# One stage of a diffusion layer: the adaLN products of a small vector with 1 MB weight slabs, in split fp32r or in plain fp32 on four column groups

## The chip, the cores and the metric

The kernel runs on one core of one Trainium2 chip. A core has a matrix engine (TensorE; PE for its matmuls and PEld for its weight loads in the profile), a vector engine (DVE), a scalar engine (ACT), GpSimd (POOL) and a queue engine (SP) that here issues nearly all transfers (DMAs). Operands lie in an on-chip memory of 128 partitions (SBUF), and matmuls write to a second one, the accumulators (PSUM). The engines run side by side, and each takes its own instructions in program order. The metric is the device time of one execution in microseconds (us), lower is better.

## The reference

The layer normalises the latent tokens `x` and the context tokens `ctx`, scales and shifts them by vectors that come from the conditioning vectors `c` and `c_ctx` (adaLN), and then does a projection, a neighbourhood attention, a short convolution and an output projection. What matters here is how scale and shift come about:

```python
def adaln(cond, w_ada, b_ada):
    m = jax.nn.silu(cond) @ w_ada + b_ada
    return jnp.split(m, 3, axis=-1)

    shift, scale, gate = adaln(c, w_ada, b_ada)
    shift_c, scale_c, gate_c = adaln(c_ctx, w_ada, b_ada)
    h = rmsnorm(x, norm_g) * (1 + scale[:, None]) + shift[:, None]
    hc = rmsnorm(ctx, norm_g) * (1 + scale_c) + shift_c
```

Here `cond` has 1024 entries, `w_ada` is 1024 x 3072 in float32, `x` is 1024 x 1024 and `ctx` 256 x 1024. Everything is float32; the kernel does its large matmuls on operands split into a high and a low part of a reduced type (fp32r).

## The kernel before

All engines are held to an order written out by hand: each instruction on PE, ACT, DVE and POOL, and each transfer of SP, is issued in the order of the program text (`strict`, line 549). So a wait at the head of one engine's queue holds everything behind it on that engine.

The stage in question is the first, lines 549 to 922. It makes the modulated activations `hh[k]`, `hl[k]` (high and low part, transposed, k = 0 to 7 blocks of 128 features) and, at the same time, the first three column groups of the projection (`first_columns`, line 723: nine matmuls of 512 columns per call, which read the high part in the first six and the low part in the last three). Two blocks k belong to one m (m = 0 to 3). For each m there are two slabs of `w_ada`, (m, 0) for shift and (m, 1) for scale, of 1024 rows x 256 columns, 1 MB each (`load_slab`, line 557). Slabs of m = 0 lie in the later places of `hh[6]`, `hh[7]`. All later ones share three buffers with the tag `slab`, and so do, in this order, the context tokens `xc` (line 835), the table `rw8` (line 736, called at line 857 as `gains_load`) and the table `rg` (line 749, in `gains`, called at line 847). A new tile takes the first buffer that comes free, so `slab` buffers pass on in this order: the buffer of (2,1) to `xc`, that of (3,0) to `rw8`, that of (3,1) to `rg`.

`products(m, j)` (line 642) multiplies silu(c), silu(c_ctx) with slab (m, j), in 8 row blocks `kt` of 128 rows, the vectors as the stationary operand and 256 columns of the slab moving. The result is 2 or 4 rows of a PSUM tile `mods[m]`, one of only two buffers named `tr`, which the transposes of x (`transposed`, line 698) and of ctx take in turn as well. Slabs (0,0), (0,1) and (1,0) are multiplied in plain fp32. For the other five, ACT (once DVE) casts the slab to a high part `slabh`, DVE subtracts to get a low part `slabl` (`cast_slab`, `rest_of`, `split`, lines 624 to 640), and PE multiplies both parts in fp32r with `c4`, whose four columns are the high and low parts of the two vectors. A slab's buffer is free once it has been split.

`row_copy` (line 653) copies the rows from PSUM; `modulation` (line 659) transposes them with four small PE transposes back into `mods[m]`, and DVE adds biases and writes the per-feature scale and shift `ab`. `turn(half, k, on)` (line 704) then makes `hh[k]`, `hl[k]` from the transposed x: ACT writes the high part `h`, ACT or DVE the full value `hw`, DVE subtracts.

In the loop over m from 1 to 3 (line 840) the order on PE is `first_columns`, `transposed`, `products(m+1, 0)`, `first_columns`, `products(m+1, 1)`, `transposed`, a third of `first_columns`, `modulation(m+1)`, the rest. `gains` stands on POOL at the head of m = 2: it scales the rope tables in `rw8` by the q and k gains into `rg`, and SP stores that (`rope_d`). Behind it on POOL stand the two powers for the norm of `xc` (`root`, line 617), for which DVE's `norm(xc)` (lines 863 and 864) waits; behind that on DVE stand `split_chunk(6)`, `modulation(3)` and the low part of `turn(1,5)`. Behind the store on SP stand the eight loads of the next weight chunks (`chunk_load(CQ, k)`, lines 848 to 900), whose casts (line 899) stand on ACT ahead of `turn(1,6)` (line 842 with m = 3).

`keep_clock(n)` (line 590) issues n idle matmuls on zeroes. After the stage, the kernel goes on to projection tiles (`pacc`, line 297), attention and the output projection.

Of the kernel before, what the change touches and what calls it, by code (L numbers as in the profile page):

```python
# [10 lines left out]
F32 = mybir.dt.float32  # L11
F32R = mybir.dt.float32r
BF16 = mybir.dt.bfloat16
AF = mybir.ActivationFunctionType
ALU = mybir.AluOpType
# [4 lines left out]
P = 128  # L20
# [3 lines left out]
KT = D // P  # L24
# [15 lines left out]
def body(tc, es, x, ctxt, w_ada, b_ada, w_in, q_g, k_g, rpbr, w_out, vecs, cst, out):  # L40
# [21 lines left out]
    pe, act, dve, pool = every = [ordered(e) for e in (nc.tensor, nc.scalar, nc.vector, nc.gpsimd)]  # L62
    sp = ordered(nc.sync)

    def sbuf(name, side=None, bufs=1):
        kw = {} if side is None else {"side": side}
        return tc.tile_pool(name=name, bufs=bufs, reuse_waits="tile", **kw)
# [43 lines left out]
    cp = es.enter_context(sbuf("cp"))  # L111
    ci = cp.tile([P, P + 2], F32, name="ci")
    ident = ci[:, 0:P]
# [15 lines left out]
    def fill_up(pool_, n):  # L129
        pool_.tile([P, n // 4], F32, name="pad")  # L130

    c2 = cp.tile([P, KT, 2], F32, name="c2")
    ab = cp.tile([P, KT, 4], F32, name="ab")
    ng, bsh, bsc = vecT[:, 16:24], vecT[:, 24:32], vecT[:, 32:40]
# [8 lines left out]
    def place(k, shape, dtype, name):  # L143

        return hpool.tile(shape, dtype, name=name, tag=f"h{k}")
# [7 lines left out]
    cvp = hs.enter_context(sbuf("cvp", side="right"))  # L153
    bp = hs.enter_context(sbuf("bp", side="right"))
    b1 = bp.tile([P, KT], F32, name="b1")
    fill_up(bp, 192)
    hcs = ExitStack()
    hcp = hcs.enter_context(sbuf("hcp"))
# [388 lines left out]
        return ps0.tile([P, 512], F32, name="tr", tag="tr", bufs=2)  # L547

    strict[:] = every + [sp]
    xx, slabs, highs, lows, chunks, mods, pts = {}, {}, {}, {}, {}, {}, {}  # L550

    def load_x(ts):
        for t in ts:
# [36 lines left out]
    def keep_clock(n):  # L590

        for _ in range(n):
            pe.matmul(acc0[2][1], warm[:, :P], warm, start=True, stop=True)
# [4 lines left out]
    dve.tensor_copy(vecT, pv[:, :nvec])  # L598
    act.activation(c2[:].rearrange("p k a -> p a k"), vecT[:, 0:16].rearrange("p (a k) -> p a k", a=2), AF.Silu)
    dve.tensor_scalar(b1, bsc, 1.0, None, ALU.add)  # L600
    c4 = cp.tile([P, KT, 4], F32R, name="c4")
    act.copy(c4[:, :, 0:2], c2)
    c0 = cp.tile([P, KT, 8], F32, name="c0")[:, :, 0:4]
    pool.memset(c0[:, :, 2:4], 0.0)
    act.copy(c0[:, :, 0:2], c2)
    keep_clock(7)
    dve.tensor_tensor(c4[:, :, 2:4], c2, c4[:, :, 0:2].bitcast(F32), ALU.subtract)

    sums = {}

# [10 lines left out]
    def norm(xtile, n):  # L621
        dve.tensor_scalar(xtile, xtile, sums[n], None, ALU.mult)

    def cast_slab(m, j, part, cast):

        if part == 0:
            highs[j] = hcp.tile([P, KT, 256], F32R, name="slabh", tag="AB"[j])
            lows[j] = place(6 + j, [P, KT, 256], F32R, "slabl")
        rows = slice(4 * part, 4 * part + 4)
        cast(highs[j][:, rows], slabs[m, j][:, rows])  # L630

    def rest_of(m, j, part):

        rows = slice(4 * part, 4 * part + 4)
        dve.tensor_tensor(lows[j][:, rows], slabs[m, j][:, rows], highs[j][:, rows].bitcast(F32), ALU.subtract)

    def split(m, j, part):

        cast_slab(m, j, part, act.copy)
        rest_of(m, j, part)  # L640

    def products(m, j, kts=range(KT), parts=(0, 1)):

        if m not in mods:
            mods[m] = tr()
        rows = mods[m][:4 if m else 2, 256 * j:256 * j + 256]
        split_ = [(c4, highs[j]), (c4, lows[j])] if (m, j) >= (1, 1) else [(c0 if m else c2, slabs[m, j])]
        for i, (c, part) in enumerate(split_):
            for kt in kts if i in parts else ():
                pe.matmul(rows, c[:, kt], part[:, kt], start=(i == 0 and kt == 0 and j == 0),  # L650
                          stop=(i == len(split_) - 1 and kt == KT - 1 and j == 1), skip_group_check=True)

    def row_copy(m):
        n = 4 if m else 2
        rw = cvp.tile([4, 512], F32, name="rw", tag="ub", bufs=2)
        (act.copy if m else dve.tensor_copy)(rw[:n], mods[m][:n])
        return rw[:n]

    def modulation(m, rw):

        n, ks = 4 if m else 2, slice(2 * m, 2 * m + 2)
        pm = mods[m]
        for j in range(2):
            for i in range(2):
                pe.transpose(pm[:, n * (2 * j + i):n * (2 * j + i + 1)], rw[:, 256 * j + i * P:256 * j + (i + 1) * P],
                             ident[:n, :n])
        both = lambda v: v[:, ks].rearrange("p (k o) -> p k o", o=1).broadcast_to([P, 2, 2])
        abk = ab[:, ks].rearrange("p k (w j) -> p j k w", w=2)
        pm = pm[:, 0:4 * n].rearrange("p (j k w) -> p j k w", j=2, k=2)
        dve.tensor_tensor(abk[:, 0], pm[:, 0, :, 0:2], both(bsh), ALU.add)  # L670
        dve.tensor_tensor(abk[:, 1], pm[:, 1, :, 0:2], both(b1), ALU.add)
        if n > 2:
            for j in range(2):
                dve.tensor_tensor(abk[:, j], abk[:, j], pm[:, j, :, 2:4], ALU.add)
        dve.tensor_tensor(abk[:, 1], abk[:, 1], both(ng), ALU.mult)

    def modulated(hi, lo, ps, k, w, on, between=None):
# [100 lines left out]
    rw = row_copy(0)  # L778
# [26 lines left out]
        norm(xx[t - 1], t - 1)  # L805
    first_columns(0, 1)
    norm(xx[7], 7)
    cast_slab(1, 1, 0, act.copy)
    cast_slab(1, 1, 1, dve.tensor_copy)
    rest_of(1, 1, 0)  # L810
    rest_of(1, 1, 1)
    products(1, 0, range(6))
    transposed(1, 0)
    products(1, 0, range(6, KT))
    turn(1, 0, act)
    load_slab(2, 1)
    load_chunks([4, 5])
    products(1, 1, parts=(0,))
    products(1, 1, range(4), (1,))
    transposed(1, 1)  # L820
    products(1, 1, range(4, KT), (1,))
    load_slab(3, 0)
    split_chunk(2)
    turn(1, 1, act)
    first_columns(1, 0)
    rw = row_copy(1)
    split_chunk(3)
    split(2, 0, 0)
    load_slab(3, 1)
    load_chunks([6, 7])  # L830
    transposed(0, 2)
    modulation(1, rw)
    turn(0, 2, dve)
    split(2, 0, 1)
    xc = sl.tile([P, 2, D], F32, name="xc", tag="slab", bufs=3)
    sp.dma_start(xc, ctxt[0].rearrange("(i p) d -> p i d", p=P))
    first_columns(1, 1)
# [2 lines left out]
    for m in range(1, 4):  # L840
        k, new, last = 2 * m, m < 3, m == 3
        turn(1, k, act)
        if m == 1:
            split(2, 1, 0)
            split(2, 1, 1)
        if m == 2:
            gkc = gains(tables)
            ch = [chunk_load(CQ, k) for k in range(4)]
        first_columns(0, k)
        transposed(0, k + 1)  # L850
        if new:
            products(m + 1, 0)
        turn(0, k + 1, dve)
        if m == 1:
            split(3, 0, 0)
            split(3, 0, 1)
            tables = gains_load()
        if m == 2:
            for i in range(2):
                square(xc[:, i], i)  # L860
            root(0)
            root(1)
            norm(xc[:, 0], 0)
            norm(xc[:, 1], 1)
        if last:
            transposed_ctx(0)
            ch[4] = chunk_split(ch[4])
            turn_ctx(0)
            spread = bias_tables()
            next(spread)  # L870
        first_columns(1, k)
        if new:
            split_chunk(k + 2)
            products(m + 1, 1)
            rw = row_copy(m + 1)
        transposed(1, k + 1)
        first_columns(0, k + 1, (0,))
        if last:
            transposed_ctx(1)
        if new:  # L880
            modulation(m + 1, rw)
        turn(1, k + 1, act)
        if new:
            split_chunk(k + 3)
        if m == 1:
            split(3, 1, 0)
        if last:
            turn_ctx(1)
        first_columns(0, k + 1, (1, 2))
        if new:  # L890
            transposed(0, k + 2)
            if m == 2:
                more_h(range(6, KT))
            turn(0, k + 2, dve)
        if m == 1:
            split(3, 1, 1)
        if m == 2:
            ch.append(chunk_load(CQ, 4))
            ch[0:4] = map(chunk_split, ch[0:4])
            ch += [chunk_load(CQ, k) for k in (5, 6, 7)]  # L900
        if last:
            group0 = conv_group(0, {u: acc0[n] for n, u in enumerate((CU, CBG, CCG))})
            next(group0)
            do_acts()
            do_dves()
            transposed_ctx(2)
            ch[5] = chunk_split(ch[5])
            turn_ctx(2)
            first_columns(1, k + 1, (0,))
            transposed_ctx(3)  # L910
            ch[6] = chunk_split(ch[6])
            first_columns(1, k + 1, (1,))
            ch[7] = chunk_split(ch[7])
            turn_ctx(3)
            first_columns(1, k + 1, (2,))
        else:
            first_columns(1, k + 1)
            transposed(1, k + 2)
# [200 lines left out]
    def both(v, n, part=slice(0, 31)):  # L1119

        lo, hi = span(2 * (n % 4))
        return v[:, :, part.start * 12:min(part.stop, hi - lo) * 12]
# [150 lines left out]
    for n in range(NT + 3):  # L1273


        p, t = divmod(n, NB)
# [51 lines left out]
        if 1 < n <= NT + 1:  # L1328
            m, r = n - 2, (n - 2) % NB
# [69 lines left out]
    with sbuf("att") as ap, psum("psb") as psb:  # L1399
# [6 lines left out]
        for n in range(len(TICKS)):  # L1406
            h, g = divmod(n, 4)
# [7 lines left out]
            if ready:  # L1415
                p = ready.pop()
# [150 lines left out]
```

## Time and profile before

| what | us |
| --- | --- |
| median of 3 runs | 630.24 |
| fastest and slowest of them | 628.92, 630.98 |
| span of the profiled execution | 629.7 |
| PE busy in it | 621.4 |
| DVE, ACT, POOL busy | 433.5, 325.5, 78.0 |
| first projection tile (`pacc`) starts at | 77.65 |

The profile is of one execution, taken on the same core; times in its views are counted from the start of its span. A row of the timeline has the start, the length, the engine, the line of the code, the operation, the tile written and the tiles read, the shapes, how many like instructions are merged, and in brackets how long the engine had been idle and what released it. "SPq" is the issue of a transfer. Nearly every instruction bears line 55, that of the helper that keeps the order; so rows are told apart by their tiles. The chain of waits is followed back from the last instruction; its rows have a start, a length and the work. A plain fp32 matmul shows up as two weight loads and two matmuls, called two passes below; an fp32r one as one of each.

### The profile page before, as it was taken

The numbers are of one execution on the slowest core, as the hardware profiler recorded it, in microseconds if no ns is written. First come the engines' busy times: TensorE is split into PE (matmuls) and PEld (weight loads), VectorE is DVE, ScalarE is ACT, GpSimd is POOL, SyncE is SP. The second block draws the span as 40 slices with busy tenths as digits, with TensorE's granted clock in tenths as the row PEclk, the third lists the DMA queues.
The fourth block names the chain that finished last, engine by engine and source line by source line (L and its number), as shares of the span: only waits on it lengthen the run. The fifth ranks groups of instructions, "written<-read, shape, count | busy, mean of one in ns | idle before, by whom it ended". The sixth has DMA issues, their size and how long they took to land.

```text
span 629.7 us, 9816 instructions
## 1 busy us (share of the span) xinstructions
PE 621.4 (99%) x3391; PEld 530.9 (84%) x3392; DVE 433.5 (69%) x889; ACT 325.5 (52%) x712; POOL 78.0 (12%) x102
## 2 busy tenths in 40 slices
PE   8999999999999999999999999999999999999998
PEld 3577899999999999888888888888878788878887
DVE  1887858866867855478897888987998755495111
ACT  4777835424625545346576568567774844451000
POOL 1305014123123222100000000000000002004200
PEclk9999999999999999999999999999999999999999
DMA  8983738967784994886566472857441235973631
GB/s 318 346 288 119 187 97 275 280 200 242 250 272 149 303 321 167 312 258 221 151 213 179 153 236 70 267 199 256 125 136 61 73 95 160 338 230 117 218 101 51
DMA packets 104030, 126.45 MB, mean 201 GB/s; under 512 B 10689, under 2 KB 70553, under 8 KB 102700
## 3 DMA queue, kind: packets, MB, share of 16 engines
q1 hardware_dynamic: 97516, 114.24, 55.3%
q10 hardware_dynamic: 6208, 11.05, 5.7%
q0 software_dynamic: 256, 0.54, 0.3%
q8 instruction: 27, 0.44, 0.3%
q14 instruction: 23, 0.19, 0.1%
HBM read 89.04 MB, written 39.04 MB: 203 GB/s over the span
## 4 chain that ended last, share of the span: by engine, by line
PE 88%; DMA 5%; ACT 3%; DVE 2%; issue 1%; ACTq 1%; SPq 1%; DVEq 0%
PE pu L55 25%; PE pacc L55 21%; PE po L55 8%; PE acc L55 6%; PE pout L76 4%; PE pout L74 4%; PE pout L75 4%; PE tr L55 4%; PE cacc L55 4%; PE pss L55 3%; DMA woraw<-in_w_out 2%; PE pc L55 2%; PE pmx L55 2%; DMA xx<-in_x 2%; DMA xr<-in_x 1%; PE trA L55 1%
## 5 line engine op out<-in xcount | busy, mean ns | idle before, releaser
L55 PE MATMUL pu<-h,uh 128*128 128x512 f32 x544 | 169.9, 394 | 0.3 <-ACT zs L55 0.3
L55 PE MATMUL pacc<-w,h 128*128 128x384 f32 x768 | 138.4, 337 | 0.0
L55 PEld LDWEIGHTS pacc<-w,h 128*128 128x128 f32 x768 | 132.7, 188 | 0.2
L55 PEld LDWEIGHTS pu<-h,uh 128*128 128x128 f32 x544 | 97.7, 188 | 17.4 <-ACT zs L55 0.6
L55 PE MATMUL pu<-h,ul 128*128 128x512 f32 x272 | 106.6, 392 | 0.0
L55 PEld LDWEIGHTS pu<-h,ul 128*128 128x128 f32 x272 | 51.1, 188 | 11.2
L55 POOL TENSOR_TENSOR ss<-ss,few 128x4 f32<-128x4 f32 (+1 forms) x40 | 41.9, 1049 | 124.8 <-DVE ss L55 124.8
L74 PE MATMUL pout<-woh,yh 128*128 128x512 f32 (+2 forms) x136 | 51.7, 380 | 1.0 <-ACT yh L1471 1.0
L75 PE MATMUL pout<-wol,yh 128*128 128x512 f32 (+2 forms) x136 | 51.6, 380 | 0.0
L76 PE MATMUL pout<-woh,yl 128*128 128x512 f32 (+2 forms) x136 | 50.9, 380 | 0.0
L55 PE MATMUL acc<-h,w 128*128 128x512 f32 x144 | 38.1, 405 | 0.8 <-ACT h L55 0.8
L55 ACT ACTIVATE sq<-pacc 128x256 f32<-128x256 f32 x32 | 12.4, 387 | 47.7 <-PE pacc L55 47.2
L55 ACT ACTIVATE phc<-sc 128x512 fp32r<-128x512 f32 x32 | 20.3, 634 | 30.1 <-DVE sc L55 30.1
L55 DVE TENSOR_REDUCE rm<-pmx 128x2 f32<-128x256 f32 (+1 forms) x33 | 13.7, 416 | 29.8 <-PE pmx L55 29.4
L55 DVE TENSOR_TENSOR mx<-mx,sb 128x372 f32<-128x372 f32 (+2 forms) x64 | 31.9, 498 | 1.9
L55 ACT COPY mg<-pmx 128x256 f32<-128x256 f32 (+1 forms) x33 | 12.0, 365 | 39.1 <-PE pmx L55 33.9
L55 PE MATMUL po<-phl,v 128*65 128x276 f32 (+2 forms) x192 | 32.0, 269 | 0.0
L55 DVE TENSOR_REDUCE ss<-sq 128x4 f32<-128x260 f32 (+1 forms) x40 | 15.6, 391 | 23.7 <-ACT sq L55 23.6
L55 ACT ACTIVATE qn<-pacc,ss 128x64 f32<-128x64 f32 x128 | 30.1, 332 | 3.0 <-POOL ss L55 3.0
L55 PEld LDWEIGHTS acc<-h,w 128*128 128x128 f32 x144 | 25.5, 188 | 6.5 <-ACT h L55 1.2
L74 PEld LDWEIGHTS pout<-woh,yh 128*128 128x128 f32 x136 | 25.6, 188 | 6.1 <-ACT yh L1471 1.5
L76 PEld LDWEIGHTS pout<-woh,yl 128*128 128x128 f32 x136 | 25.6, 188 | 5.1 <-DVE yl L1472 0.4
(159 smaller groups left out, 1158.7 us busy)
## 6 DMA issues: line engine op xcount, KB each, us to landing
uraw<-in_w_in SPq DMA_DIRECT2D x34, 256.0 KB
q_d<-qs SPq DMA_DIRECT2D x32, 256.0 KB
k_s<-k_d SPq DMA_DIRECT2D x8, 1024.0 KB
q_s<-q_d SPq DMA_DIRECT2D x16, 512.0 KB
wr<-in_w_in SPq DMA_DIRECT2D x40, 192.0 KB
slab<-in_w_ada SPq DMA_DIRECT2D x6, 1024.0 KB
v_d<-vs SPq DMA_DIRECT2D x20, 260.0 KB
v<-v_d SPq DMA_DIRECT2D x16, 325.0 KB
```

The lines of the kernel that those rows point to most:

```text
L55: i = emit(*a, **kw)
L74: i = pe.matmul(ps, ah, bh, start=first, stop=False)
L75: pe.matmul(ps, ah, bl, start=False, stop=False)
L76: pe.matmul(ps, al, bh, start=False, stop=last)
```

## The change

All eight slabs are multiplied in plain fp32, unsplit. The stationary operand is `c32`: 32 columns, of which two hold the vectors and 30 are zero. Row block `kt` writes to output partitions 32·(kt mod 4) to 32·(kt mod 4) + 31, so consecutive row blocks go to four different groups of 32 partitions, and each group holds a partial sum over two row blocks. `row_copy` copies all 128 partitions; the four partial sums are added in `modulation` by four matmuls with a selector, two columns of the constant `ci` with ones at partitions of one parity, in place of the four transposes. Casts and subtractions of the slabs go, with them `c4`, `c0`, `slabh`, `slabl`. The products of slabs (1,0) and (1,1), which stood in pieces between transposes, now stand whole ahead of both transposes.

```diff
+    fill_up(cp, 128)
+    c32 = cvp.tile([P, KT, 32], F32, name="c32", tag="cv", bufs=2)
+    pool.memset(c32, 0.0)
+    act.copy(c32[:, :, 0:2], c2)
...
-        rows = mods[m][:4 if m else 2, 256 * j:256 * j + 256]
-        split_ = [(c4, highs[j]), (c4, lows[j])] if (m, j) >= (1, 1) else [(c0 if m else c2, slabs[m, j])]
-        for i, (c, part) in enumerate(split_):
-            for kt in kts if i in parts else ():
-                pe.matmul(rows, c[:, kt], part[:, kt], start=(i == 0 and kt == 0 and j == 0),
-                          stop=(i == len(split_) - 1 and kt == KT - 1 and j == 1), skip_group_check=True)
+        for kt in range(KT):
+            g = 32 * (kt % 4)
+            pe.matmul(mods[m][g:g + 32, 256 * j:256 * j + 256], c32[:, kt], slabs[m, j][:, kt],
+                      start=(j == 0 and kt < 4), stop=(j == 1 and kt >= 4), skip_group_check=True)
...
+        for n in range(4):
+            pe.matmul(pm[:, 2 * n:2 * n + 2], rw[:, n * P:(n + 1) * P], ci[:, P:P + 2], start=True, stop=True)
...
-        if n > 2:
-            for j in range(2):
-                dve.tensor_tensor(abk[:, j], abk[:, j], pm[:, j, :, 2:4], ALU.add)
...
-    cast_slab(1, 1, 0, act.copy)
-    cast_slab(1, 1, 1, dve.tensor_copy)
-    rest_of(1, 1, 0)
-    rest_of(1, 1, 1)
-    products(1, 0, range(6))
+    products(1, 0)
+    products(1, 1)
     transposed(1, 0)
-    products(1, 0, range(6, KT))
     turn(1, 0, act)
     load_slab(2, 1)
     load_chunks([4, 5])
-    products(1, 1, parts=(0,))
-    products(1, 1, range(4), (1,))
     transposed(1, 1)
-    products(1, 1, range(4, KT), (1,))
...
         turn(0, k + 1, dve)
         if m == 1:
-            split(3, 0, 0)
-            split(3, 0, 1)
             tables = gains_load()
```

The other six calls of `split` go in the same way.

More of the change, by code (lines that the diff above doesn't have):

```diff
@@ L549, in body @@
     strict[:] = every + [sp]
-    xx, slabs, highs, lows, chunks, mods, pts = {}, {}, {}, {}, {}, {}, {}
+    xx, slabs, chunks, mods, pts = {}, {}, {}, {}, {}
     def load_x(ts):
@@ L600, in body @@
     dve.tensor_scalar(b1, bsc, 1.0, None, ALU.add)
[L601 to L605, printed above, removed]
+    fill_up(cp, 128)
+    c32 = cvp.tile([P, KT, 32], F32, name="c32", tag="cv", bufs=2)
+    pool.memset(c32, 0.0)
+    act.copy(c32[:, :, 0:2], c2)
     keep_clock(7)
-    dve.tensor_tensor(c4[:, :, 2:4], c2, c4[:, :, 0:2].bitcast(F32), ALU.subtract)
     sums = {}
@@ L622, in norm @@
         dve.tensor_scalar(xtile, xtile, sums[n], None, ALU.mult)
[L624 to L642, printed above, removed]
+    def products(m, j):
         if m not in mods:
             mods[m] = tr()
-        rows = mods[m][:4 if m else 2, 256 * j:256 * j + 256]
-        split_ = [(c4, highs[j]), (c4, lows[j])] if (m, j) >= (1, 1) else [(c0 if m else c2, slabs[m, j])]
-        for i, (c, part) in enumerate(split_):
-            for kt in kts if i in parts else ():
-                pe.matmul(rows, c[:, kt], part[:, kt], start=(i == 0 and kt == 0 and j == 0),
-                          stop=(i == len(split_) - 1 and kt == KT - 1 and j == 1), skip_group_check=True)
+        for kt in range(KT):
+            g = 32 * (kt % 4)
+            pe.matmul(mods[m][g:g + 32, 256 * j:256 * j + 256], c32[:, kt], slabs[m, j][:, kt],
+                      start=(j == 0 and kt < 4), stop=(j == 1 and kt >= 4), skip_group_check=True)
@@ L653, in row_copy @@
     def row_copy(m):
[L654 to L657, printed above, removed]
+        rw = cvp.tile([P, 512], F32, name="rw", tag="ub", bufs=2)
+        (act.copy if m else dve.tensor_copy)(rw, mods[m])
+        return rw
     def modulation(m, rw):
-        n, ks = 4 if m else 2, slice(2 * m, 2 * m + 2)
+        ks = slice(2 * m, 2 * m + 2)
         pm = mods[m]
-        for j in range(2):
-            for i in range(2):
-                pe.transpose(pm[:, n * (2 * j + i):n * (2 * j + i + 1)], rw[:, 256 * j + i * P:256 * j + (i + 1) * P],
-                             ident[:n, :n])
+        for n in range(4):
+            pe.matmul(pm[:, 2 * n:2 * n + 2], rw[:, n * P:(n + 1) * P], ci[:, P:P + 2], start=True, stop=True)
@@ L667, in modulation @@
         both = lambda v: v[:, ks].rearrange("p (k o) -> p k o", o=1).broadcast_to([P, 2, 2])
         abk = ab[:, ks].rearrange("p k (w j) -> p j k w", w=2)
-        pm = pm[:, 0:4 * n].rearrange("p (j k w) -> p j k w", j=2, k=2)
-        dve.tensor_tensor(abk[:, 0], pm[:, 0, :, 0:2], both(bsh), ALU.add)
-        dve.tensor_tensor(abk[:, 1], pm[:, 1, :, 0:2], both(b1), ALU.add)
-        if n > 2:
-            for j in range(2):
-                dve.tensor_tensor(abk[:, j], abk[:, j], pm[:, j, :, 2:4], ALU.add)
+        pm = pm[:, 0:8].rearrange("p (j k w) -> p j k w", j=2, k=2)
@@ L675, in modulation @@
+        dve.tensor_tensor(abk[:, 0], pm[:, 0], both(bsh), ALU.add)
+        dve.tensor_tensor(abk[:, 1], pm[:, 1], both(b1), ALU.add)
         dve.tensor_tensor(abk[:, 1], abk[:, 1], both(ng), ALU.mult)
@@ L827, in body @@
     split_chunk(3)
-    split(2, 0, 0)
     load_slab(3, 1)
@@ L833, in body @@
     turn(0, 2, dve)
-    split(2, 0, 1)
     xc = sl.tile([P, 2, D], F32, name="xc", tag="slab", bufs=3)
@@ L842, in body @@
         turn(1, k, act)
-        if m == 1:
-            split(2, 1, 0)
-            split(2, 1, 1)
         if m == 2:
@@ L884, in body @@
             split_chunk(k + 3)
-        if m == 1:
-            split(3, 1, 0)
         if last:
@@ L894, in body @@
             turn(0, k + 2, dve)
-        if m == 1:
-            split(3, 1, 1)
         if m == 2:
```

## The prediction

> **What bounds the kernel now.** I read the page's head first, then the chain of waits in order of time, then the timeline of the first 80 us.
>
> ```profile
> span 629.7 us, 9816 instructions
> ...
> PE 621.4 (99%) x3391; PEld 530.9 (84%) x3392; DVE 433.5 (69%) x889; ACT 325.5 (52%) x712; POOL 78.0 (12%) x102
> ```
>
> PE is busy almost throughout, and the other engines have room. So work taken from DVE and ACT is worth something only where PE waits for them, and a new wait of PE lengthens the run by its whole length. The chain shows where each microsecond of the first stage goes:
>
> ```profile
> 4.99 9.87 DMA xx<-in_x
> ...
> 25.24 6.60 PE tr L55 x40
> 31.84 2.07 PE acc L55 x9
> 33.91 0.77 PE tr L55 x8
> 34.68 2.27 PE acc L55 x9
> 36.95 0.44 PE tr L55 x4
> 37.39 2.54 PE acc L55 x9
> 39.92 2.26 PE tr L55 x20
> 42.19 2.06 PE acc L55 x9
> ...
> 54.19 2.26 PE tr L55 x20
> 56.45 2.06 PE acc L55 x9
> 58.51 2.31 PE tr L55 x20
> ...
> 68.49 0.91 PE tr L55 x8
> ...
> 77.65 12.51 PE pacc L55 x72
> ```
>
> "acc" is `first_columns`; "tr" holds transposes and products. Up to about 15 us the chain is the load of x; from 25 us it is PE alone. A "tr x20" is four transposes (0.44 as at 36.95) and sixteen product passes, so one split slab costs PE 2.26 - 0.44 = 1.82 (after (2,1) and (3,1): 2.31 - 0.44 = 1.87). Last comes what waits beside PE and is nearly late already:
>
> ```profile
> 40.59 2.36 DVE L55 TENSOR_TENSOR slabl<-slab,slabh 128x1024 fp32r<-128x1024 f32 x2
> 42.98 0.37 SPq L55 DMA_DIRECT2D xc<-in_ctx  x1
> 44.31 2.35 DVE L55 TENSOR_TENSOR slabl<-slab,slabh 128x1024 fp32r<-128x1024 f32 x2
> 46.70 0.34 SPq L55 DMA_DIRECT2D rw<-in_q_norm_g  x1
> 47.56 0.42 SPq L55 DMA_DIRECT2D rw<-in_cst  x1
> 52.04 1.35 DVE L55 TENSOR_TENSOR slabl<-slab,slabh 128x1024 fp32r<-128x1024 f32 x1
> 53.47 5.95 POOL L55 TENSOR_TENSOR rg<-rw 128x512 f32<-128x512 f32 x4 [1.16 <-DVE slabl L55]
> 59.44 0.33 SPq L55 DMA_DIRECT2D rope_d<-rg  x1
> 59.81 8.39 SPq L55 DMA_DIRECT2D wr<-in_w_in  x8
> 59.98 1.58 DVE L55 TENSOR_SCALAR xc<-xc,xss 128x1024 f32<-128x1024 f32 x2 [2.07 <-POOL xss L55]
> 65.11 2.24 ACT L55 CAST w<-wr 128x384 fp32r<-128x384 f32 x4 [0.41 <-DMA wr<-in_w_in]
> 67.93 0.77 ACT L55 ACTIVATE hw<-tr,ab 128x512 f32<-128x512 f32 x1
> 68.75 0.42 PEld L55 LDWEIGHTS tr<-ci,xc 128*128 128x128 f32 x4
> ```
>
> Three hand-overs of a slab buffer are visible: the second low part of (2,1) ends at 42.95 and `xc` is issued at 42.98; that of (3,0) ends at 46.66 and the loads of `rw8` start at 46.70; that of (3,1) ends at 53.39 and POOL starts on `rg` at 53.47. From there one chain runs on: `rg` ends at 59.42, the store goes at 59.44, the chunk loads behind it, their casts on ACT start at 65.11 after a wait for the DMA, then `turn(1,6)`, whose last ACT part ends at 68.70, and at 68.75 PE takes the context transposes, which need the `tr` buffer that it frees. PE came from 68.49 without a break, so this side chain has about 0.1 us of slack.
>
> **The change, part by part.**
>
> *The price S of a slab on PE.* Four groups of output partitions at once is an operation that the trace doesn't show. These rows bound it:
>
> ```profile
> L55 PE MATMUL tr<-slab,c x48: 378/379/380, 6.7 to 29.1; 128*2 128x256 f32 x32, 128*4 128x256 f32 x16
> ...
> 6.71 7.07 PE L55 MATMUL tr<-slab,c 128*2 128x256 f32 x32
> ...
> 27.69 1.05 ACT L55 CAST slabh<-slab 128x1024 fp32r<-128x1024 f32 x1 [2.61 <-DMA slab<-in_w_ada]
> ...
> 28.64 0.77 ACT L55 ACTIVATE h<-tr,ab 128x512 fp32r<-128x512 f32 x1
> ...
> 34.27 0.40 PE L55 MATMUL tr<-ci,rw 4*128 4x4 f32 x4
> ```
>
> The first row is from the view by tile, the others from the timeline. 32 plain passes take 7.07; a pass by itself takes 379 ns, so 31 intervals fill 6.69, 0.216 each. Sixteen in a row without overlap are S = 3.45; four at a time S = 0.86. Both passes of one row block use the same 32 output partitions and follow each other directly. If PE keeps their order, only the second pass of a block can run beside the first of the next: nine steps of 0.216, S = 1.94. I take 2.0, since two passes per block are what the row shows, and keep 0.86 and 3.45 as ends. That is no better than the 1.82 of a split slab. The Trainium skill, "TensorE: Matmul & The Clock Gate", Part 3, has matmuls in different column groups overlap, a pack lasting as long as one matmul and 4 ns for each further tile, but also says that matmuls start and end in strict order; no run here shows either yet. Taken for all four groups, it gives the lower end.
>
> *`modulation`.* Four transposes (0.33 of the 0.77 at 33.91) become four plain matmuls, eight passes. At the transposes' pace they take 0.66, at that of full 128-row transposes (0.44 for four) 0.88: I take +0.45 for each m. Two small DVE additions go and nothing on PE waits for them.
>
> *Products ahead of the transposes.* (1,1) lands by 27.69, where ACT's wait for it ends; (1,0) can be multiplied from 25.24 and ends before that for S up to 2.45. Then come S, `transposed(1,0)` 0.44, `h` 0.77, `hw` 0.77 and `transposed(1,1)` 0.44, which needs the `tr` buffer that `turn(1,0)` reads (the other is `mods[1]`), and 0.15 for hand-overs. `first_columns(1,0)` starts at 30.26 + S instead of 31.84: S - 1.58. The pieces of products that covered this wait are gone.
>
> *Up to `products(3,0)`.* To 37.39: 2.07 + 0.44 + 0.78 + 2.07 + 0.44 = 5.80 for 5.55, +0.25. At 37.39 a block took 2.54 for 2.07, waiting for DVE, which no longer subtracts slabs: -0.46. Then (2,0) S - 1.82, (2,1) S - 1.87, `modulation(2)` +0.45, (3,0) S - 1.82. Sum: 4S - 6.85. With S = 2.0, +1.15: `products(3,0)` ends at 57.6 instead of 56.45.
>
> *Casts and subtractions removed.* Ten subtractions of 1.2 us and ten casts leave DVE and ACT. Beyond the 0.46, PE waited for none of them, so they are worth nothing more. Products of m = 0 end before the load of x at 14.86 in any case: nothing.
>
> *Who frees the buffers.* This decides. A slab's buffer came free when DVE had split it; now when PE has multiplied it, and PE multiplies (3,0) one stage later: 57.6 instead of 46.66. `rw8` is loaded from there. How long that takes:
>
> ```profile
> 47.00:48.00 1.00, 1.00 (x8) 0.76 (x7) 0.44 (x5) 1.00 (x3) 0.00 (x0) 1.00 0.95 389
> ...
> 50.00:51.00 1.00, 1.00 (x6) 0.83 (x5) 1.00 (x2) 1.00 (x2) 0.20 (x1) 1.00 0.60 196
> 51.00:52.00 1.00, 1.00 (x9) 0.82 (x8) 0.96 (x2) 0.36 (x1) 0.71 (x2) 1.00 0.81 324
> 52.00:53.00 1.00, 1.00 (x7) 0.83 (x6) 1.00 (x2) 0.83 (x2) 0.31 (x1) 1.00 0.08 33
> ```
>
> The last two columns, DMA share and GB/s, show earlier loads until about 48 and then the 0.5 MB table until about 52.1, which is 5.4 after 46.70. Without loads ahead of it, up to 1.3 of this (46.70 to 48) could go, which leaves 4.1. I take 4.8, as little else moves at 57 but the small loads keep their latency, and 4.1 and 5.4 as ends. So `rg` starts at 57.6 + 4.8 = 62.4 (`products(3,1)` ends earlier, at 57.6 + 2.07 + 2.0 = 61.7) and ends at 68.4, 9.0 later than 59.42. Everything behind moves with it: on DVE `norm(xc)`, `split_chunk(6)`, `modulation(3)` and the low part of `turn(1,5)`, for which PE's third part of `first_columns(1,5)` waits; on SP the store and the eight chunk loads; on ACT their casts and `turn(1,6)`; on PE the context transposes. The two gates aren't added: the later one, with 0.1 slack, gives +8.9. After it PE works without a break into `pacc`, so nothing takes it back.
>
> *The clock.* PE would stand still for some 5 us from about 67, between its last work that needs nothing of DVE and the late low part of `turn(1,5)`.
>
> ```profile
> 1.38 2.74 PE L55 MATMUL acc<-warm 128*128 128x512 bf16 x6 [1.38 <-POOL c L55]
> ...
> 16.70 1.24 PE L55 MATMUL acc<-warm 128*128 128x512 bf16 x5
> ```
>
> At the start of the run a matmul takes 0.46, later 0.25, though the granted clock reads 1.00 in both. If PE slowed down again, its 3.7 us of work between the two gates would take up to 1.7 longer, inside a gap of some 5 us before the second gate: nothing in the sum, up to +1.7 in the range. The Trainium skill, "TensorE: Matmul & The Clock Gate", Part 1, states that an idle window of some 3.4 us halves the clock; the row of the start agrees with nearly a factor of two, and by that rule the 1.7 would be spent there.
>
> **Sum.** 629.7 + 8.9 = 638.6 of span; the median lies 0.5 above the profiled span, so 639.1.
>
> **The rivals.**
> (a) Four groups overlap fully, S = 0.86: `products(3,0)` ends at 53.0, `rg` at 63.8, +4.3: 634.5, or 633.8 with the quick load. For it: the four groups share nothing in PSUM. Against it: the two passes per block.
> (b) The groups don't overlap, so the change doesn't do what it says, S = 3.45: (1,0) and (1,1) end at 32.1, `first_columns(1,0)` starts at 34.7 (+2.9), then 3 x 3.45 - 5.27 = +5.1, `products(3,0)` ends at 64.4. `rg` waits for (3,1) until 69.9 and ends at 75.9: +16.3, 646.5.
> (c) The buffers aren't handed on as I read it (a table finds another free one), and PE's own sum decides: 4S - 6.85 plus S - 1.87 for (3,1) plus 0.45, or 5S - 8.27. It turns at S = 1.65. With S = 0.86 it is -4.0: 626.3, faster. Against it are the three hand-overs within 0.1 us of each other.
> (d) The same with S = 2.0: +1.7, 632.0.
>
> **How the numbers follow.** The forecast has 0.48, (a) 0.24, (b) 0.16, (c) 0.06, (d) 0.06. The range runs from (a) with the quick load and a little less, 633.0, to (b) with some loss of clock, 647.5; it leaves out (c) and (d). About 0.3%, 1.9 us, is what a measurement of this kernel can tell from no change: faster 0.06 (c), same 0.02 (the edge of d), slower 0.92.
>
> **What would show it.** Right: the loads of `rw8` are issued within 0.1 us of the last matmul on slab (3,0), near 57.6; `rg` ends near 68.4; DVE waits for POOL ahead of `norm(xc)` for over 5 us; `pacc` starts near 86.5. S is read from the eight products of a slab: 2.0, or 0.9, or 3.5. Wrong: `rw8` loaded before 50 us, or a first stage in which PE has no gap over 2 us.

## The result and the profile after

| | before | after |
| --- | --- | --- |
| median, us | 629.88 (4 runs, 628.92 to 630.98) | 636.78 (4 runs, 636.23 to 638.74) |
| span of the profiled execution | 629.7 | 634.5 |
| PE busy in it | 621.4 | 616.6 |
| DVE, ACT busy | 433.5, 325.5 | 420.4, 318.0 |
| projection tiles (`pacc`) start | 77.65 | 83.80 |

The ratio of after to before is 1.0121, with a 95% interval of 1.0100 to 1.0143. (The row before has one run more than the table ahead of the prediction.) PE has 4.8 us less to do, DVE 13.1 and ACT 7.5, and the run is 6.9 us longer.

The head of the page after the change:

```profile
span 634.5 us, 9820 instructions
...
PE 616.6 (97%) x3408; PEld 529.5 (83%) x3408; DVE 420.4 (66%) x871; ACT 318.0 (50%) x702; POOL 76.8 (12%) x102
```

The chain of waits after the change, in order of time (start, length, work):

```profile
31.28 2.08 PE acc L55 x9
33.37 1.23 PE tr L55 x12
...
39.31 1.44 PE tr L55 x20
...
52.62 1.48 PE tr L55 x20
54.12 0.34 SPq L55
...
54.98 5.09 DMA rw<-in_cst
...
60.23 4.97 POOL rg L55 x4
65.21 1.35 POOL xss L55 x2
...
68.07 0.70 DVE h L55
...
68.81 1.65 PE acc L55 x3
70.45 0.85 PE tr L55 x4
71.31 3.35 PE acc L55 x9
74.66 0.45 PE tr L55 x4
...
83.80 12.51 PE pacc L55 x72
```

Before, this stretch was PE alone. Now the chain leaves PE at 54.1, where the last product of slab (3,0) frees its buffer, and goes through SP, a table load of 5.09, POOL's `rg` of 4.97, the powers and DVE, until PE goes on at 68.81. A slab with its four transposes takes 1.44 (39.31) where it took 2.26. So S, the price of a slab on PE, is 1.44 - 0.44 = 1.0 for slab (2,0); by the same reckoning it is 1.04 for (3,0) (52.62) and 1.15 for (2,1) (1.59 at 43.02).

The timeline shows the waits of the three engines that the late tables hold up, and one slab's products. What stands in brackets is the idle time before and what ended it:

```profile
52.98 1.07 PE L55 MATMUL tr<-slab,c 128*32 128x256 f32 x16
54.12 0.34 SPq L55 DMA_DIRECT2D rw<-in_q_norm_g  x1
...
65.77 1.58 DVE L55 TENSOR_SCALAR xc<-xc,xss 128x1024 f32<-128x1024 f32 x2 [9.43 <-POOL xss L55]
68.81 1.65 PE L55 MATMUL acc<-h,w 128*128 128x512 f32 x3 [6.07 <-DVE h L55]
70.89 2.23 ACT L55 CAST w<-wr 128x384 fp32r<-128x384 f32 x4 [1.87 <-DMA wr<-in_w_in]
70.96 3.70 PE L55 MATMUL acc<-h,w 128*128 128x512 f32 x9
```

The products of (3,0) end at 54.05 and the table's loads start at 54.12. Before, they started at 46.70, behind DVE's subtraction. DVE's wait for POOL grew from 2.07 to 9.43 us, and PE, which never stood still here, stands still for 6.07.

Two waits of PE hang on the late tables; they are called the two gates below. The first is the one of 6.07: PE needs the low part `h` of `turn(1,5)`, which stands on DVE behind `norm(xc)`, which waits for POOL. The second is PE's wait ahead of the context transposes for the buffer that `turn(1,6)` frees: `turn(1,6)` stands on ACT behind the casts of the weight chunks (70.89), whose loads stand on SP behind the store of `rg`. In this execution the first gate decides: `turn(1,6)` ends on ACT at 74.47, and PE, slow behind its gap, comes to the context transposes only about 0.3 us after that.

The two profiled executions differ by 4.8 in span and by 6.15 at `pacc`. The execution of before that the prediction used was longer than most: a second one (`e9` below) has a span of 627.6 and `pacc` at 76.94, and against that both differences are 6.9, as in the medians.

### The profile page after: what moved, and what is told of

Read it like the earlier page. It is cut to its first block, busy times and chain, and to the rows that moved or that the text cites. A ratio compares the mean times of both kernels' runs of the same rounds, so it can differ in the third digit from the quotient of the medians.

```text
span 634.5 us, 9820 instructions
## 1 busy us (share of the span) xinstructions
PE 616.6 (97%) x3408; PEld 529.5 (83%) x3408; DVE 420.4 (66%) x871; ACT 318.0 (50%) x702; POOL 76.8 (12%) x102
## 4 chain that ended last, share of the span: by engine, by line
PE 89%; DMA 3%; DVE 3%; ACT 2%; POOL 1%; issue 1%; SPq 1%; ACTq 0%; POOLq 0%; DVEq 0%
PE pu L55 27%; PE pacc L55 21%; PE po L55 8%; PE pout L76 5%; PE pout L74 5%; PE pout L75 5%; PE acc L55 4%; PE cacc L55 3%; PE pss L55 3%; PE tr L55 2%; PE pc L55 2%; PE pmx L55 2%; DMA xx<-in_x 1%; PE trA L55 1%; DMA rw<-in_cst 1%
## 5 line engine op out<-in xcount | busy, mean ns | idle before, releaser
L55 PE MATMUL acc<-h,w 128*128 128x512 f32 x144 | 40.5, 423 | 6.8 <-DVE h L55 6.1
L55 PEld LDWEIGHTS acc<-h,w 128*128 128x128 f32 x144 | 26.9, 199 | 13.5 <-DVE h L55 6.8
```

Of the source, the lines that this page charges most:

```text
L55: i = emit(*a, **kw)
```

## The experiments

Each was timed against the kernel before on the same chip; the ratio is given with its 95% interval where there were enough runs.

### The tables in buffers of their own

```diff
-        rw = sl.tile([P, 2048], F32, name="rw8", tag="slab", bufs=3)
+        rw = hcp.tile([P, 2048], F32, name="rw8", tag="A")
...
-        rg = sl.tile([P, 2, NB, 2, HD], F32, name="rg", tag="slab", bufs=3)
+        rg = hcp.tile([P, 2, NB, 2, HD], F32, name="rg", tag="B")
```

(Tags A and B held `slabh` before the change; nothing is in them now until the context is turned.)

> The changed kernel, with the two rope tables put into two buffers that nothing else uses at that time, instead of the slab buffers of (3,0) and (3,1). Theory (the loss is the late hand-over of the slab buffers): the loads of the table are issued near 45 us instead of 54, DVE no longer waits 9 us for POOL, PE has no gap of 6 us near 63, the projection tiles start near 75 instead of 83.6, and the time falls to about 627, under the kernel before. Rival 1 (the products in column groups, or the selector, make the stage longer by themselves): the time stays at 633 or more. Rival 2 (the time lost is PE's slower clock, not the tables): the gap shrinks, but less than half of the 7 us comes back.

Measured: 632.36 us, ratio 1.0036 (1.0013 to 1.0060). From the timeline:

```profile
57.88 0.33 SPq L55 DMA_DIRECT2D rope_d<-rg  x1
58.42 1.58 DVE L55 TENSOR_SCALAR xc<-xc,xss 128x1024 f32<-128x1024 f32 x2 [2.82 <-POOL xss L55]
...
64.99 1.97 ACT L55 CAST w<-wr 128x384 fp32r<-128x384 f32 x4 [3.31 <-DMA wr<-in_w_in]
...
68.36 1.04 PE L55 MATMUL tr<-ci,xc 128*128 128x128 f32 x4 [3.00 <-ACT hw L55]
```

The gap of 6 us near 63 is gone, and 4.4 of the 6.9 us are back. The expected 627 is missed (and with it 75 for the projection tiles, which start at 78.65), because the second gate stayed: the chunk loads still stand behind the tables' store on SP, the first chunk lands only at 64.97, and now that PE is 3 us ahead, it waits those 3.00 us for ACT's `turn(1,6)`. Rival 1 is out; rival 2 too, since more than half came back.

### The kernel before with late buffers

```diff
+        if m == 3:
+            pe.matmul(mods[m][32:36, 256 * j:256 * j + 256], c0[:, 7], slabs[m, j][:, 7], start=(j == 0), stop=(j == 1), skip_group_check=True)
```

> The kernel before, unchanged in its split slabs, but with one more small plain matmul behind the products of (3,0) and of (3,1), which reads the slab as loaded and writes to rows that nobody reads; so the buffers of (3,0) and (3,1) come free only when PE has passed there. Theory: the table's loads are issued near 57 instead of 46.7, the tables are ready near 68.5 instead of 59.4, and the time is about 639, some 9 us over the kernel before, though only about 0.9 us of PE work is added. Rival (the late hand-over costs little, the loss comes from the products themselves): about 631.

Measured: 639.81 us, ratio 1.0141 (1.0102 to 1.0179). From its timeline:

```profile
54.97 0.59 PE L55 MATMUL tr<-slab,c 128*4 128x256 f32 x2
55.60 0.34 SPq L55 DMA_DIRECT2D rw<-in_q_norm_g  x1
...
67.44 1.58 DVE L55 TENSOR_SCALAR xc<-xc,xss 128x1024 f32<-128x1024 f32 x2 [10.94 <-POOL xss L55]
```

The added matmul ends at 55.56, the load goes at 55.60, DVE then waits 10.94 for POOL. Two small matmuls, of some 0.5 us each on PE, cost 10 us: the late hand-over alone, with the split slabs as they were, makes a loss larger than that of the change. This is the strongest evidence for the cause.

### The price of a slab: two groups, one group, pairs

```diff
-            g = 32 * (kt % 4)
+            g = 32 * (kt % 2)     # e3_two_groups
+            g = 0                 # e4_one_group
+            g = 32 * (kt // 2)    # e7_pairs
```

(The copy and the sum take as many rows as are written; start and stop flags follow the groups.)

> The changed kernel with the row blocks in turn on two groups (output partitions 0 and 32) instead of four; 64 rows are copied and summed. If each group takes one matmul at a time and the groups run side by side, the sixteen passes of a slab take 8 x 0.216 = 1.7 us instead of 1.0, products of (3,0) end near 57 and the time is about 640. If 1.0 is the pace of issue (sixteen passes at 62 ns) and the groups don't matter, the passes take 1.0 and the time stays at 637.

> The changed kernel with all row blocks on one group (output partitions 0 to 31). Theory: nothing overlaps, a slab takes 16 x 0.216 = 3.45 us, products of (3,0) end near 65.5, the tables are ready near 76.6 and the time is about 648, which is rival (b) of the prediction. If the pace of issue sets 1.0 the time stays at 637.

> The changed kernel with consecutive row blocks in pairs on one group: output partitions 0, 0, 32, 32, 64, 64, 96, 96. If passes start strictly in their order and wait for their group, only the changes of group overlap: about 13 x 0.216 = 2.8 us for a slab, and about 645. If each group works off its own passes whatever stands between them in the order, 1.0 us and about 637.

Measured: 640.80 us (two runs, ratio 1.0167, 1.0121 to 1.0213), 647.69 (two runs, 1.0276, 1.0231 to 1.0322) and 635.93 in one run. The products of slab (2,0), from the timelines of the three, in this order:

```profile
40.61 1.92 PE L55 MATMUL tr<-slab,c 128*32 128x256 f32 x16
```

```profile
43.05 3.64 PE L55 MATMUL tr<-slab,c 128*32 128x256 f32 x16
```

```profile
39.62 1.09 PE L55 MATMUL tr<-slab,c 128*32 128x256 f32 x16
```

With the last pass's own 0.38 taken off, fifteen intervals fill 1.54, 3.26 and 0.71: 0.103, 0.217 and 0.047 each. That is 0.216 by the number of groups (0.108, 0.216, 0.054) within 0.01. Pairs cost what alternating groups cost, although a pair puts four passes of one group behind one another. The single passes of the pairs start in four bunches of four, at 39.62, 39.86, 40.08 and 40.29. Passes on one group start 0.216 apart in `e4`, so a bunch can only hold one pass of each group. So each group works off its own passes, whatever stands between them in the program, and the strict order that the forecast built on isn't there. (That each engine takes its instructions in program order, as said at the start, is too strong here for PE.) The time follows S: from two groups to one, S grows by 1.72 and the time by 6.9, four times as much, as the sum's 4S says; from four groups to two the two are 0.85 and 4.0.

### The two gates, and the clock

`e5_chunks_first` takes the chunk loads out from behind the store and leaves the tables late. `e6_filled_gap` leaves both and gives PE work in the gap.

```diff
-            gkc = gains(tables)
             ch = [chunk_load(CQ, k) for k in range(4)]
+            gkc = gains(tables)
```

> The changed kernel with the first four chunk loads issued on SP ahead of the store of the tables, with which they have nothing to do; the tables stay in the slab buffers. Two gates hang on the late tables: DVE's wait for POOL, which holds the low part that PE's first_columns(1,5) needs, and the chunk loads behind the store, which hold turn(1,6) on ACT. Theory (not additive, and after the first gate PE is slow long enough to arrive at the second on time anyway): DVE still waits 9 us for POOL, the gap of PE stays at 6 us, and at most 0.5 us comes back, 636 to 637. Rival (the chunk loads are the gate that counts): 632 or less.

```diff
+        if m == 2:
+            pts[0, 6] = tr()
+            for _ in range(6):
+                pe.matmul(pts[0, 6][:], ident, xx[0][:, 0:512], start=True, stop=True)
```

> The changed kernel with six plain matmuls of 512 columns ahead of transposed(0,6), into the tile that this transpose then overwrites: 5.2 us of PE work in the gap of 6 us, which computes nothing. Theory (the tables decide and the second gate stands behind): the passes after the gap take 0.23 again instead of 0.4 to 0.55, but PE then waits for turn(1,6) near 74.5, and the time falls by 1 us at most, to about 636. Rival (PE's slower clock after the gap is a loss of its own): the 3 us that the blocks after the gap took longer come back, about 634.

Measured: 638.62 us (1.0143, 1.0130 to 1.0156) and 638.18 (1.0128, 1.0107 to 1.0148). Neither is under the changed kernel, and both miss the 636 or 637 that was expected. From the timeline of `e5`, then of `e6`:

```profile
54.31 0.34 SPq L55 DMA_DIRECT2D rw<-in_q_norm_g  x1
...
61.77 4.95 POOL L55 TENSOR_TENSOR rg<-rw 128x512 f32<-128x512 f32 x4 [0.99 <-DMA wr<-in_w_in]
...
67.27 1.58 DVE L55 TENSOR_SCALAR xc<-xc,xss 128x1024 f32<-128x1024 f32 x2 [10.73 <-POOL xss L55]
...
70.31 1.65 PE L55 MATMUL acc<-h,w 128*128 128x512 f32 x3 [7.37 <-DVE h L55]
```

```profile
62.59 5.31 PE L55 MATMUL tr<-xx,ci 128*128 128x512 f32 x12
...
71.77 2.33 PE L55 MATMUL acc<-h,w 128*128 128x512 f32 x9
...
76.36 0.66 PE L55 MATMUL tr<-ci,xc 128*128 128x128 f32 x4 [1.81 <-ACT hw L55]
```

In `e5` the first gate alone holds PE for 7.37 us. The edit also has a price: the chunk loads now go out right behind the table's, and `rg` starts 7.46 us after the first of the table's loads (54.31 to 61.77), where the changed kernel took 6.11; the likely reason is that the loads share the DMAs. From the end of `rg` to `pacc`, `e5` takes 84.70 - 66.72 = 17.98 us, and the changed kernel 83.80 - 65.20 = 18.60. So in these two profiles the open second gate is worth 0.6 us, and the later tables lose 1.35.

In `e6` the filling works: the nine matmuls at 71.77 take 2.33, where after the gap of the changed kernel they took 3.70 (its row at 70.96). But most of what PE gains it waits for at 76.36. The loads of the tables began 1.8 us later in the profiled run of `e6` than in that of the changed kernel, before the edit acts, so the two are compared from the end of the tables to `pacc`. Chain of `e6`:

```profile
62.07 4.95 POOL rg L55 x4
...
85.07 5.05 PE pacc L55 x29
```

That is 85.07 - 67.02 = 18.05 in `e6` and 18.60 in the changed kernel. So in these profiles the slow passes after the gap cost 0.55 us, not the 3 of the rival; the rest of their time is hidden by the second gate, which opens about then. In the medians no gain shows, and the ranges overlap (636.07 to 639.31 for `e6`). The two gates don't add up: with the first one shut, the second is worth next to nothing, and with the first one gone (`e1`), the second still holds PE for 3.00 us.

### Both gates open

`e8_both_mended` joins the edits of `e1` and `e5`, loads the tables ahead of slab (3,1) (`tables = gains_load()` moved up) and has `keep_clock(12)` for `keep_clock(2)` behind the products of m = 0. `e10_reordered` adds:

```diff
     products(1, 0)
-    products(1, 1)
     transposed(1, 0)
     turn(1, 0, act)
...
+    products(1, 1)
+    first_columns(1, 0, (0,))
     transposed(1, 1)
...
-    first_columns(1, 0)
+    first_columns(1, 0, (1, 2))
```

> The changed kernel with the tables in buffers of their own and loaded ahead of slab (3,1), the first four chunk loads ahead of the tables' store, and ten more idle matmuls behind the products of slab (0,1), so that PE doesn't stand still before 13 us. Theory: neither DVE nor ACT waits for the tables or for chunks behind them, PE has no gap over 2 us after 20 us, its passes keep their pace, the projection tiles start near 74 instead of 83.6, and the time is 626 to 627.5, under both kernels. Rival (the plain products and the selector themselves make the stage longer than the split ones): not under 630.

> e8_both_mended with the products of (1,1) moved behind transposed(1,0), and a third of first_columns(1,0) ahead of transposed(1,1), so that PE has work while ACT turns the first block. Theory (what e8 still loses to the kernel before is PE's wait for slab (1,1) and for ACT near 30 us): first_columns(1,0) starts near 29.5 instead of 31.5, the projection tiles start near 73.5, and the time is 627 to 628.5, some 1.5 to 2 us less than e8. Rival (what e8 loses lies in the start, in the load of x and the clock, and differs from run to run): within 0.7 us of e8.

Measured: 629.64 us, ratio 1.0004 (0.9984 to 1.0023), and 626.72, ratio 0.9957 (0.9943 to 0.9972). `e8` misses its 626 to 627.5, and `e10` comes in just under its 627 to 628.5. From its timeline, and then from that of `e10`:

```profile
27.69 1.07 PE L55 MATMUL tr<-slab,c 128*32 128x256 f32 x16 [1.14 <-DMA slab<-in_w_ada]
...
30.89 0.66 PE L55 MATMUL tr<-ci,xx 128*128 128x128 f32 x4 [1.54 <-ACT hw L55]
```

```profile
28.13 0.33 PE L55 MATMUL tr<-ci,xx 128*128 128x128 f32 x1 [0.87 <-DVE xx L55]
28.39 1.07 PE L55 MATMUL tr<-slab,c 128*32 128x256 f32 x16
29.39 0.96 PE L55 MATMUL acc<-h,w 128*128 128x512 f32 x3
```

The products moved together leave PE waiting for slab (1,1) and then for `turn(1,0)`, 2.7 us in all; in `e10` it waits 0.87. That the whole difference of 2.9 us between the two medians comes from there isn't shown. The runs of `e8` lie between 627.96 and 633.71, and its profiled one, of 628.17, was among the shortest; that of `e10`, of 628.10, was among its longer ones. In these two profiles `e10` reaches `pacc` 1.0 us earlier (74.34 for 75.35), but the spans are alike (626.3 and 626.4): `e10` then waits 1.0 us for ACT in the output projection, and `e8` 0.3.

### Controls on the kernel before

> The kernel before once more, for a second profile of it: how far its span, its load of x and its first stage differ from one execution to the next. Theory: the tables' loads follow the low part of slab (3,0) within 0.1 us again and the projection tiles start within 1.5 us of 77.65; the output projection's wait of 1.0 us for ACT needn't be there again, and then the span is about 628.5.

> The kernel before, with split slabs, and only the first four chunk loads issued on SP ahead of the tables' store: the half of the mending that the kernel before can take, since its spare buffers hold the split slabs. Theory: in the kernel before PE sets the pace of the stage and the side chain has 0.1 us of slack, so nothing is won: within 0.3% of 629.9. Rival (what e10 wins comes from this order of the loads and not from the shorter products): 627 to 628.

`e9` is unchanged and took 629.46 in one run, with a span of 627.6; the wait of 1.0 us that PE had for ACT in the output projection of the first profile isn't there this time. Chain of `e9`, then of `e10`:

```profile
76.94 7.13 PE pacc L55 x41
```

```profile
74.34 9.73 PE pacc L55 x56
```

The mended kernel reaches the projection tiles 2.6 us ahead of the kernel before, which is most of the 3.2 us between the medians. `e11` has only the edit of `e5`, on the kernel before: 629.75, ratio 0.9997 (0.9988 to 1.0006). So the order of the loads is worth nothing where PE sets the pace. What `e10` wins fits the shorter products, once nothing waits for the tables: the prediction's sum for PE alone, 5S - 8.27, gives -3.3 with S = 1.0, and 3.2 was measured. But the early tables, the idle matmuls and the new order of `e10` weren't tried on the kernel before, so this is argued and not shown.

## Why the prediction was right, and where it was off

- **The cause** holds. The buffers of (3,0) and (3,1) are handed on when PE has read them, the table's loads follow within 0.07 us, and POOL, DVE, SP and ACT are late in turn. `e2` shows it by itself, `e1` by taking it away. Rivals (c) and (d), a table that finds another buffer, are out.
- **The price of a slab** was mis-sized: 2.0 in the forecast, 1.0 measured. The step that failed is the strict order of the two passes of a row block; `e7` shows that groups don't keep it. So rival (a) had the right overlap, close to its 0.86: four bunches of 0.216 are 0.86, and the rest of the 1.0 goes by between these products and the matmuls around them. Rival (b), one group, is what `e4` makes: it was given 646.5 and measured 647.69.
- **Up to `products(3,0)`**: with S = 1.0 the sum 4S - 6.85 gives -2.85, an end at 53.6; measured 54.05. `first_columns(1,0)` starts at 31.28, and the formula has 31.26, but that is luck: the formula counts from the landing of slab (1,1), while PE here had multiplied both slabs by about 27.9 and then waited 0.35 for DVE to normalise the last rows of x (28.76). `modulation` was right too: 1.23 for transposes and selector at 33.37, so 0.79 for 0.33, +0.46 for +0.45.
- **The table's load** was put at 4.8 and took 6.1 (54.12 to 60.23), more than the upper end of 5.4, although the DMAs had moved nothing else since 50 us; why it took so long stays open. `rg` then took 4.97 for 5.95. Together the two came to 11.1 for a forecast of 10.75. `rg` ends at 65.20, 5.8 later than before. The forecast had 9.0: S made it 4.0 too late, and the end of `products(3,0)` and the tables 0.8 too early.
- **The gates**: they aren't added, as said, but the one that decides is not the one that was named. The prediction took the second gate for the later one. The slower passes after the gap, which it allowed for in the range (up to 1.7) and not in the sum, took PE 0.3 us past the second gate, so that the first gate and these passes decide, and `pacc` moved by 6.15 where the tables moved by 5.8.
- **The whole**: +8.9 was forecast and +6.9 measured. With S = 1.0 in place of 2.0 the working gives +4.9, and what it lacked is spread over the end of `products(3,0)` (0.45), the way through the tables (0.35) and the second gate (0.4); the remaining 0.8 is put down to the first profile's base, as `e9` reaches `pacc` 0.7 earlier. So it is partly luck that 639.1 came within 2.3 us of the measured 636.78: an S twice too large and the smaller terms that were missed went opposite ways.

## What to carry to other kernels

When a computation that freed a buffer early is removed, look for who takes that buffer next, and follow that work to the end: here 13 us less on DVE and shorter products cost 7 us, through a table that had nothing to do with either. If PE has two waits that hang on one late transfer, opening one of them shows less than the whole: the tables moved out of the way gave back 4.4 of 6.9 us (`e1`), and the second gate alone nothing (`e5`). Only with both open did the kernel with the shorter products come out ahead (626.72 for 629.89).

## What the runs showed of the hardware

- Plain fp32 products of 32 columns on different groups of 32 output partitions overlap in full: 3.64, 1.92 and 1.07 us for sixteen passes on one, two and four groups, and 1.09 with the groups in pairs. The Trainium skill, "TensorE: Matmul & The Clock Gate", Part 3, has the overlap, and the 1.07 agrees; it also has matmuls start and end in strict order, which the pairs' 1.09 doesn't bear out for passes that belong to different groups.
- PE was slower after gaps of some 2 us and less. Near 13 us in the changed kernel it had stood still for 0.94, 0.70 and 2.03 us, with short products between:

```profile
8.62 0.64 PE L55 MATMUL tr<-slab,c 128*32 128x256 f32 x8 [0.94 <-DMA slab<-in_w_ada]
9.95 0.64 PE L55 MATMUL tr<-slab,c 128*32 128x256 f32 x8 [0.70 <-DMA slab<-in_w_ada]
...
13.16 1.87 PE L55 MATMUL tr<-ci,rw 128*128 128x2 f32 x8 [2.03 <-DVE rw L55]
...
16.12 2.34 PE L55 MATMUL acc<-warm 128*128 128x512 bf16 x5
```

  The five matmuls at 16.12 take 0.47 each, those at 16.70 before took 0.25, and the eight of the selector 1.87 where they take 0.95 later. The granted clock of the changed kernel says so. In the rows below, each stretch has its length, the busy time of PE, PEld, DVE, ACT and POOL with the number of instructions, and then the granted clock: 0.86 in the first row, and 0.86 in the third, which holds the gap of 6.07. After that gap nine matmuls take 3.35 (71.31 in the chain) where they took 2.08 before. In the kernel before all three stretches read 1.00, though its very first matmuls take 0.46 too, so the granted clock doesn't tell all. `e10`, with ten more idle matmuls near 13 us, reads 1.00 in the first stretch. Whether the length of a gap counts or the share of idle time isn't shown.

```profile
0.00:25.00 25.00, 19.18 (x91) 9.91 (x92) 8.81 (x23) 13.64 (x24) 5.25 (x14) 0.86 0.94 347
25.00:60.00 35.00, 33.11 (x243) 24.45 (x242) 15.22 (x31) 18.89 (x31) 3.45 (x5) 1.00 0.60 208
60.00:84.00 24.00, 17.87 (x83) 14.23 (x83) 14.90 (x30) 12.67 (x25) 6.72 (x15) 0.86 0.59 162
```

- A load of 0.5 MB, with only the two small loads of the same table issued up to 0.86 us ahead of it, landed 5.09 us after its issue (54.98). The DMAs had moved nothing from 50 to 55 us.
